# Gate and up weights of an FFN loaded in one piece into free residual buffers, last sums in place, two more places for weight forms

## The chip, the core and the metric

The kernel runs on one core of a Trainium2 chip: TensorE (PE) multiplies, VectorE (DVE), ScalarE (ACT) and GpSimd (POOL) do the rest, and SyncE (SP) issues the DMAs from one queue that is worked off in order. Each engine, too, works through its own list in order. The metric is the device time of one execution in microseconds: the median of three runs of the kernel before is 1670.28 (1666.36 to 1670.28).

## The reference

One decoder layer over 1024 tokens of width 1024, in float32: a mixer (eight retention heads beside four differential-attention heads), a memory cross-attention with four heads, and a SwiGLU feed-forward with 2816 hidden columns. All sub-layers are residual behind an RMS norm. The change touches the last of them:

```python
h = rms_norm(x, norm_ffn[l])
x = x + (jax.nn.silu(h @ w_gate[l]) * (h @ w_up[l])) @ w_down[l]
```

## The kernel before

Each float32 operand is split into a rounded high part and the rest as a low part, and a product is three matmuls (high by high, high by low, low by high) that add up in PSUM. The feed-forward saves one product in eight by a Strassen-Winograd scheme: operands are cut into quarters, sums of the quarters are formed, and seven products f1 to f7 take the place of eight.

The token side (`b_sums`, `b_part`) is prepared while the cross-attention ends. For each group p of 256 tokens the normed rows `xn_f` (L772) are summed (`bs`, L829), transposed by TensorE (`bt`) and split (`Bh`, `Bl`, `B4` to `B6`, L849 and L89).

The gate/up loop then runs over 22 hidden blocks j of 128 columns. `Forms(j)` (L1019) loads the raw gate and up block, 512 KB each, into two of the three buffers of the pool `st`; `sums` (L1033) builds sums of quarters in `sa` and `sb` on VectorE; `form` (L1028) turns each of the seven operands into a high part (a cast on ScalarE, L1030) and a low part (a subtraction, L89, on GpSimd or for f6 and f7 on VectorE). All seven go into the pool `w` with nine places. `GU.prod` issues the twelve matmuls of one product and `GU.after` (L1098) takes results out of PSUM: ScalarE copies one PSUM bank (`U` L1107, `G` L1112 and L1116), VectorE adds the other (`G`, `U`, L1013), ScalarE applies SiLU, GpSimd multiplies the second half of `G` (L1121) and VectorE the first (L1123). In one step TensorE's order is product 1 of block j+1, 7 of j, 2 of j+1, 4 of j, 5, 6 and 3 of j+1. Banks of one PSUM tile `xz` hold several products, so product 5 waits for the add that ends product 2, product 7 for the add that ends product 3, and product 6 for the copy `U` of product 5.

After every second block `g_forms` (L1068) forms the activations' sums `gSa` and `gSb` (tiles of the pool `xn`, two places) and stores them to `gF_d`. Also every second block `w_forms` (L1050) loads two raw blocks of the down weights into `st`, forms four sums in two tiles `wTa` and `wTb` of the pool `t4` (six places), and stores them to `wT_d`. The down projection behind the loop reads both back (`ds`), splits and multiplies them, and adds the residual, which was saved in `res_d` and is loaded into four 1 MB tiles `res` of the pool tag "B". Two of the four B places hold `B4` through the loop; the other two are free once the residual rows that were in them are normed.

TensorE's order is the order of the code. For the other engines and the DMA queue a scheduler chooses the order at build time: it takes whichever instruction it thinks ready first, with the earlier in the code preferred, and hands out pool places as they come free. A change of pools therefore moves instructions on every engine but TensorE.

Of the kernel before, what the change touches and what calls it, by code (L numbers as in the profile page):

```python
# [9 lines left out]
F32 = mybir.dt.float32  # L10
F32R = mybir.dt.float32r
# [5 lines left out]
P = 128  # L17
# [13 lines left out]
U_RET, U_DIF, U_OUT, U_KV, U_XQ, U_XO, U_GU, U_DN = 0, 16, 28, 36, 52, 60, 68, 112  # L31
# [6 lines left out]
def body(ctx, tc, a, out):  # L38
    nc = tc.nc
    ve, sc, gp, sp = nc.vector, nc.scalar, nc.gpsimd, nc.sync  # L40
# [15 lines left out]
    up = ctx.enter_context(tc.tile_pool(name="up", bufs=NW))  # L56
# [3 lines left out]
    drp = ctx.enter_context(tc.tile_pool(name="drp", bufs=1, space=bass.MemoryType.DRAM))  # L60
# [4 lines left out]
    def t4(name, dt=F32):  # L65
        return tp4.tile([P, 1024], dt, tag="t4", name=name)
# [20 lines left out]
    def low(eng, dst, src, hi):  # L87

        eng.tensor_tensor(out=dst, in0=src, in1=hi.bitcast(F32), op=ALU.subtract)  # L89

    def raw(name):
        return stp.tile([P, 1024], F32, tag="st", name=name)
# [173 lines left out]
    for i in range(2):  # L266
        r = c1.tile([P, P], F32, tag=f"R{i}", name=f"R{i}")
# [38 lines left out]
    class Ret:  # L306
        def __init__(self, g, w):
            self.g, self.w = g, w
            self.msk = c1.tile([P, 2, P], F32, tag="msk", bufs=2, name=f"msk{g}")
            sp.dma_start(self.msk, a["msk"][:, g])  # L310
            self.xi = c1.tile([P, P], F32, tag="xi", bufs=2, name=f"xi{g}")
            sp.dma_start(self.xi, a["xi"][:, g])
            self.o, self.rg = t4b(f"ro{g}"), t4b(f"rg{g}")
            self.st = {}
# [437 lines left out]
    bp = p2.enter_context(tc.tile_pool(name="bp", bufs=1))  # L752
    xr2 = [bp.tile([P, 2, D], F32, tag="B", bufs=4, name=f"xr{t}") for t in range(4)]
    xr = [xr2[t // 2][:, t % 2] for t in range(NT)]
    xnp = p2.enter_context(tc.tile_pool(name="xnp", bufs=2))
# [7 lines left out]
    def xnp_tile(name):  # L763
        return xnp.tile([P, 1024], F32, tag="xn", name=name)

    def normed(t, grow, name, pool=None):

        r = small(1, "rn", f"r_{name}")
        xn = (pool or xnp_tile)(f"xn_{name}")
        sc.activation(xn, xr[t], AF.Square, accum_out=r)  # L770
        rsqrt(r, 1, 1.0 / D, name)
        ve.scalar_tensor_tensor(out=xn, in0=xr[t], scalar=r, in1=grow, op0=ALU.mult, op1=ALU.mult)  # L772
        return xn
# [26 lines left out]
    for c in range(2):  # L800
        u = [unit(U_OUT + 4 * c + i, f"wo{c}_{i}", eng=ve if i % 2 else gp, pool=ntp if c and i < 2 else None)
             for i in range(4)]
        for t in range(NT):
# [8 lines left out]
            xn = normed(t, grow, f"x{t}", pool=t4 if t % 2 else None)  # L812
# [199 lines left out]
    def add(eng, dst, x, y):  # L1012
        eng.tensor_tensor(out=dst, in0=x, in1=y, op=ALU.add)  # L1013

    def sub(eng, dst, x, y):
        eng.tensor_tensor(out=dst, in0=x, in1=y, op=ALU.subtract)  # L1016


    class Forms:  # L1019
        def __init__(self, j):  # L1020
            self.j, self.fs = j, {}
            self.g, self.u = (raw(f"gu{j}_{i}") for i in range(2))
            sp.dma_start(self.g, a["w"][U_GU + 2 * j])
            sp.dma_start(self.u, a["w"][U_GU + 2 * j + 1])
            self.form(1, self.g[:, 0:512], gp)
            self.form(2, self.g[:, 512:1024], gp)

        def form(self, f, src, eng):  # L1028
            self.fs[f] = t = up.tile([P, 2, 512], F32R, tag="w", name=f"f{f}_{self.j}")
            sc.copy(t[:, 0], src)  # L1030
            low(eng, t[:, 1], src, t[:, 0])

# [15 lines left out]
    wT = {}  # L1048

    def w_forms(p):  # L1050

        r1, r2 = (raw(f"wd{p}_{i}") for i in range(2))
        for i, r in enumerate((r1, r2)):
            sp.dma_start(r, a["w"][U_DN + 2 * p + i])
        x, y = t4(f"wTa{p}"), t4(f"wTb{p}")
        B11, B12, B21, B22 = r1[:, 0:512], r1[:, 512:1024], r2[:, 0:512], r2[:, 512:1024]
        sub(ve, x[:, 0:512], B12, B11)
        sub(ve, x[:, 512:1024], B22, x[:, 0:512])
        sub(ve, y[:, 0:512], B22, B12)
        sub(ve, y[:, 512:1024], B21, x[:, 512:1024])  # L1060
        d = drp.tile([2, P, 1024], F32, tag=f"wT{p}", name=f"wT_d{p}")
        sp.dma_start(d[0], x)
        sp.dma_start(d[1], y)
        wT[p] = d

    gF, Gs = {}, {}

    def g_forms(p):  # L1068

        g1, g2 = Gs.pop(2 * p), Gs.pop(2 * p + 1)  # L1070
        A11, A21, A12, A22 = g1[:, 0:512], g1[:, 512:1024], g2[:, 0:512], g2[:, 512:1024]
        x, y = xnp_tile(f"gSa{p}"), xnp_tile(f"gSb{p}")
        d = drp.tile([4, P, 1024], F32, tag=f"gF{p}", name=f"gF_d{p}")
        sp.dma_start(d[0][:, 0:512], A11)
        sp.dma_start(d[1], g2)
        add(ve, x[:, 0:512], A21, A22)
        sub(ve, x[:, 512:1024], x[:, 0:512], A11)
        sub(ve, y[:, 0:512], A11, A21)
        sub(ve, y[:, 512:1024], A12, x[:, 512:1024])
        sp.dma_start(d[2], x)  # L1080
        sp.dma_start(d[3], y)
        gF[p] = d

    class GU:
# [13 lines left out]
        def after(self, f, c=slice(0, 512)):  # L1098
            X, Z = self.xz[:, c], self.xz[:, 512 + c.start:512 + c.stop]
            if self.G is None and f == 2:  # L1100
                self.G = t4(f"G{self.j}")
            if self.U is None and f == 5:
                self.U = hfp.tile([P, 512], F32, tag="xsq" if self.j % 2 else "xp", bufs=1, name=f"U{self.j}")
            if f == 1 or f in (6,) or (f != 5 and self.G is None):
                return
            if f == 5:
                sc.copy(self.U[:, c], Z)  # L1107
                return
            G1, G2 = self.G[:, c], self.G[:, 512 + c.start:512 + c.stop]
            U = self.U[:, c] if self.U is not None else None  # L1110
            if f == 2:
                sc.copy(G1, self.y[:, c])  # L1112
                add(ve, G1, X, G1)
                sc.activation(G1, G1, AF.Silu)
            if f == 3:
                sc.copy(G2, Z)  # L1116
                add(ve, G2, X, G2)
                sc.activation(G2, G2, AF.Silu)
            if f == 7:
                add(ve, U, X, U)  # L1120
                gp.tensor_tensor(out=G2, in0=G2, in1=U, op=ALU.mult)  # L1121
            if f == 4:
                ve.tensor_tensor(out=G1, in0=X, in1=G1, op=ALU.mult)  # L1123
                Gs[self.j] = self.G
                if self.j % 2 and c.stop == 512:
                    g_forms(self.j // 2)
# [31 lines left out]
    for j in range(NH):  # L1158
        n = GU(j + 1) if j + 1 < NH else None
        if n:  # L1160
            n.forms.sums()
            n.go(1)
        o.go(7, c1 if j == 0 else call_)
        if n:
            n.go(2)
        o.go(4, c1 if j == 0 else call_)
        if j % 2 == 0:
            w_forms(j // 2)
        if n:
            n.go(5)  # L1170
            n.prod(6)
            n.go(3)
        o = n
# [6 lines left out]
    X = [xs_[i // 2][:, 512 * (i % 2):512 * (i % 2) + 512] for i in range(4)]  # L1180
    Y = [(mm, ms)[i // 2](f"dy{i}") for i in range(4)]
    gsrc = {1: (0, 0), 2: (1, 0), 4: (1, 1), 5: (2, 0), 6: (2, 1), 7: (3, 0), 3: (3, 1)}
    wsrc = {5: (0, 0), 6: (0, 1), 7: (1, 0), 4: (1, 1)}

    outs = {1: [(X, 0, 0)], 2: [(Y, 0, 0, 1)], 6: [(X, 0, 1)], 5: [(Y, 1, 1)], 7: [(X, 1, 1, 1)],
            3: [(Y, 0, 1, 1)], 4: [(X, 1, 0, 1)]}
# [1 line left out]
    for f in (1, 2, 6, 5, 7, 3, 4):  # L1188
        bank = Y if f in (2, 5, 3) else X
        for p in range(NP):  # L1190
            s_ = raw(f"ds{f}_{p}")
            d, x = gsrc[f]
            sp.dma_start(s_[:, 0:512], gF[p][d][:, h5_(x)])
            if f in wsrc:
                d, x = wsrc[f]
# [10 lines left out]
        for b_, e, c, *last in outs[f]:  # L1206
            for i in range(4):
                t = 2 * i + e
# [74 lines left out]
def build(arrays):  # L1283
    nc = bacc.Bacc("TRN2", target_bir_lowering=False, num_devices=1, dynamic_dma_scratch_size=1024)
    aps = {k: nc.dram_tensor(f"in_{k}_dram", v.shape, mybir.dt.from_np(v.dtype), kind="ExternalInput").ap()
           for k, v in arrays.items()}
    out = nc.dram_tensor("out_0_dram", (NT, P, D), F32, kind="ExternalOutput").ap()
    with tile.TileContext(nc) as tc:
        with ExitStack() as ctx:
            body(ctx, tc, aps, out)  # L1290
    return nc
# [10 lines left out]
```

## Time and profile before

| | |
|---|---|
| median of three runs | 1670.28 us |
| the profiled execution | 1660.91 us, of it 1659.1 between first and last instruction |
| mean granted TensorE clock in it | 0.985 |
| busy: TensorE, VectorE, ScalarE, GpSimd | 93%, 60%, 37%, 25% |
| entry to the loop | about 941 to 1012 us |
| gate/up loop, steps 1 to 20 | 1012.49 to 1430.26 us |
| down projection | 1446.20 us to the end |

The page gives shares over the whole span, where stages have different limits. A change of one stage is read from the rows of that stage: what TensorE waited for there, and what chain of work ended that wait. The start of product 6 (the one behind the `U` copy) marks a step well, because TensorE always stops there for a moment. In the rows by stretch, what stands behind the length is the busy time of TensorE, of its weight loads (PEld), of VectorE, ScalarE and GpSimd, each with its count of instructions, and then the granted TensorE clock, the DMA engines' busy share and GB/s.

### The profile page before, as it was taken

The numbers are of one execution on the slowest core, as the hardware profiler recorded it, in microseconds if no ns is written. First come the engines' busy times: TensorE is split into PE (matmuls) and PEld (weight loads), VectorE is DVE, ScalarE is ACT, GpSimd is POOL, SyncE is SP. The second block draws the span as 40 slices with busy tenths as digits, with TensorE's granted clock in tenths as the row PEclk, the third lists the DMA queues.
The fourth block names the chain that finished last, engine by engine and source line by source line (L and its number), as shares of the span: only waits on it lengthen the run. The fifth ranks groups of instructions, "written<-read, shape, count | busy, mean of one in ns | idle before, by whom it ended". The sixth has DMA issues, their size and how long they took to land.

```text
span 1659.1 us, 23264 instructions
## 1 busy us (share of the span) xinstructions
PE 1549.4 (93%) x8712; PEld 1317.8 (79%) x8712; DVE 995.7 (60%) x2473; ACT 616.5 (37%) x1187; POOL 421.7 (25%) x343
## 2 busy tenths in 40 slices
PE   6899899899899999899999869999999999899998
PEld 5778878878888878798998767777777777788887
DVE  8955864864866724766676884444444444455554
ACT  5542442442445522332332443333333333333332
POOL 4323223223303411111121234433333333100000
PEclk8999999999999999999999989999999999999999
DMA  8201011111104552100011133444444444576664
GB/s 283 71 26 52 31 39 39 44 39 39 40 14 140 192 177 77 39 26 26 26 64 37 67 115 131 143 148 144 143 146 144 144 146 146 197 238 217 195 221 155
DMA packets 68417, 180.84 MB, mean 109 GB/s; under 512 B 7632, under 2 KB 13136, under 8 KB 68304
## 3 DMA queue, kind: packets, MB, share of 16 engines
q1 hardware_dynamic: 67296, 178.81, 31.6%
q8 instruction: 68, 1.11, 0.3%
q10 hardware_dynamic: 1008, 0.55, 0.1%
q14 instruction: 45, 0.37, 0.1%
HBM read 135.55 MB, written 43.78 MB: 108 GB/s over the span
## 4 chain that ended last, share of the span: by engine, by line
PE 63%; DVE 21%; DMA 6%; ACT 4%; issue 3%; POOL 3%; SPq 0%; POOLq 0%; ACTq 0%; DVEq 0%
PE xz L47 12%; PE g_r L47 8%; PE dx L47 7%; PE dy L47 5%; PE wo L47 5%; PE xo L47 5%; PE xq L47 4%; PE kv L47 3%; DMA gu<-in_w_dram 3%; PE q L47 2%; PE y L47 2%; PE av L47 2%; DVE sb L1016 1%; PE rsk L47 1%; DVE nmx L522 1%
## 5 line engine op out<-in xcount | busy, mean ns | idle before, releaser
L47 PE MATMUL xz<-Bh,f 128*128 128x512 f32 (+1 forms) x552 | 173.3, 386 | 7.5 <-DVE G L1013 7.4
L47 PE MATMUL g_r<-uh_r,xT 128*128 128x512 f32 x512 | 178.9, 407 | 0.0
L89 DVE TENSOR_TENSOR dl<-ds,dh 128x1024 fp32r<-128x1024 f32 x77 | 94.3, 1224 | 102.5 <-PE dy L47 36.7
L1200 ACT CAST dh<-ds 128x1024 fp32r<-128x1024 f32 x77 | 81.1, 1053 | 138.8 <-DMA ds<-wT_d 57.0
L47 PEld LDWEIGHTS xz<-Bh,f 128*128 128x128 f32 x552 | 103.0, 189 | 32.6 <-DVE G L1013 12.4
L47 PE MATMUL kv<-uh_d,xT 128*128 128x256 f32 x512 | 113.0, 303 | 5.4 <-DVE dql L445 5.4
L47 PEld LDWEIGHTS g_r<-uh_r,xT 128*128 128x128 f32 x512 | 97.0, 189 | 22.3 <-issue 2.5
L89 POOL TENSOR_TENSOR f<-gu,f 128x512 fp32r<-128x512 f32 x66 | 87.6, 1341 | 106.4 <-ACT f L1030 106.4
L47 PE MATMUL xz<-Bl,f 128*128 128x512 f32 (+1 forms) x276 | 105.3, 382 | 0.0
L47 PE MATMUL g_r<-ul_r,xT 128*128 128x512 f32 x256 | 101.0, 395 | 0.0
L47 PEld LDWEIGHTS kv<-uh_d,xT 128*128 128x128 f32 x512 | 88.8, 201 | 8.0 <-DVE dql L445 5.6
L47 PE MATMUL xq<-hT,uh_xq 128*128 128x256 f32 x512 | 94.4, 286 | 0.0
L47 PE MATMUL xo<-uh_xo,xoT 128*128 128x512 f32 x256 | 89.7, 409 | 2.1 <-DVE B6l L89 1.6
L525 ACT ACTIVATE p<-s,nmx,dsm 128x128 f32<-128x128 f32 (+7 forms) x64 | 53.2, 832 | 97.1 <-DVE nmx L523 96.4
L47 PEld LDWEIGHTS xq<-hT,uh_xq 128*128 128x128 f32 x512 | 81.1, 195 | 0.0
L47 PE MATMUL xz<-B6h,f 128*128 128x512 f32 (+1 forms) x184 | 61.4, 397 | 17.7 <-ACT U L1107 17.7
L47 PE MATMUL kv<-ul_d,xT 128*128 128x256 f32 x256 | 75.1, 293 | 2.4 <-DVE ul_d L89 2.4
L47 PE MATMUL xq<-hT,ul_xq 128*128 128x256 f32 x256 | 73.1, 285 | 0.0
L47 PE MATMUL dx<-dh 128*128 128x512 f32 x176 | 68.6, 390 | 0.4 <-DVE G L1123 0.4
L89 POOL TENSOR_TENSOR f<-sa,f 128x512 fp32r<-128x512 f32 x22 | 33.6, 1525 | 139.2 <-issue 77.4
L47 PE MATMUL dx<-dl,dh 128*128 128x512 f32 x176 | 68.5, 389 | 0.0
L47 PE MATMUL dx<-dh,dl 128*128 128x512 f32 x176 | 68.5, 389 | 0.0
(333 smaller groups left out, 4125.5 us busy)
## 6 DMA issues: line engine op xcount, KB each, us to landing
gu<-in_w_dram SPq DMA_DIRECT2D x44, 512.0 KB, 3.7
ds<-gF_d SPq DMA_DIRECT2D x77, 256.0 KB, 3.9
wd<-in_w_dram SPq DMA_DIRECT2D x22, 512.0 KB, 4.0
ds<-wT_d SPq DMA_DIRECT2D x44, 256.0 KB, 4.3
ds<-in_w_dram SPq DMA_DIRECT2D x33, 256.0 KB, 4.0
st_r<-in_w_dram SPq DMA_DIRECT2D x16, 512.0 KB, 3.3
st_kv<-in_w_dram SPq DMA_DIRECT2D x16, 512.0 KB, 3.4
st_d<-in_w_dram SPq DMA_DIRECT2D x12, 512.0 KB, 3.4
```

The costliest lines, as they stand in the source:

```text
L47: return tc.keep_in_program_order(nc.tensor.matmul(*args, **kw))
L89: eng.tensor_tensor(out=dst, in0=src, in1=hi.bitcast(F32), op=ALU.subtract)
L522: ve.tensor_reduce(out=nmx[:, m:m + 1], in_=s[:, :n], axis=AX.X, op=ALU.max, negate=True)
L525: sc.activation(pt[:, :n], s[:, :n], AF.Exp, bias=nmx[:, m:m + 1], scale=rq[:, m:m + 1], accum_out=Z[:, m:m + 1])
L1016: eng.tensor_tensor(out=dst, in0=x, in1=y, op=ALU.subtract)
L1200: sc.copy(hi, s_)
```

## The change

Three edits. The raw gate and up blocks of j >= 1 come as one load into one B place instead of two `st` buffers; block 0 stays as it was. The forms f3 and f7 of j >= 1 go into the two places of `xn`, whose former users `gSa` and `gSb` move to `t4`. `w_forms` makes its four sums in place, in the `st` buffers that were loaded, so `t4` loses `wTa` and `wTb`; the four sums land in another order, hence the new `wsrc`.

```diff
--- before.py
+++ after.py
@@ -1019,14 +1019,20 @@
     class Forms:
         def __init__(self, j):
             self.j, self.fs = j, {}
-            self.g, self.u = (raw(f"gu{j}_{i}") for i in range(2))
-            sp.dma_start(self.g, a["w"][U_GU + 2 * j])
-            sp.dma_start(self.u, a["w"][U_GU + 2 * j + 1])
+            if j:
+                gu = bp.tile([P, 2, 1024], F32, tag="B", bufs=4, name=f"gu{j}")
+                self.g, self.u = gu[:, 0], gu[:, 1]
+                sp.dma_start(gu, a["w"][U_GU + 2 * j:U_GU + 2 * j + 2].rearrange("i p c -> p i c"))
+            else:
+                self.g, self.u = (raw(f"gu{j}_{i}") for i in range(2))
+                for i, t in enumerate((self.g, self.u)):
+                    sp.dma_start(t, a["w"][U_GU + 2 * j + i])
             self.form(1, self.g[:, 0:512], gp)
             self.form(2, self.g[:, 512:1024], gp)
 
         def form(self, f, src, eng):
-            self.fs[f] = t = up.tile([P, 2, 512], F32R, tag="w", name=f"f{f}_{self.j}")
+            pool, tag = (xnp, "xn") if self.j and f in (3, 7) else (up, "w")
+            self.fs[f] = t = pool.tile([P, 2, 512], F32R, tag=tag, name=f"f{f}_{self.j}")
             sc.copy(t[:, 0], src)
             low(eng, t[:, 1], src, t[:, 0])
 
@@ -1049,19 +1055,17 @@
 
     def w_forms(p):
 
-        r1, r2 = (raw(f"wd{p}_{i}") for i in range(2))
-        for i, r in enumerate((r1, r2)):
-            sp.dma_start(r, a["w"][U_DN + 2 * p + i])
-        x, y = t4(f"wTa{p}"), t4(f"wTb{p}")
-        B11, B12, B21, B22 = r1[:, 0:512], r1[:, 512:1024], r2[:, 0:512], r2[:, 512:1024]
-        sub(ve, x[:, 0:512], B12, B11)
-        sub(ve, x[:, 512:1024], B22, x[:, 0:512])
-        sub(ve, y[:, 0:512], B22, B12)
-        sub(ve, y[:, 512:1024], B21, x[:, 512:1024])
-        d = drp.tile([2, P, 1024], F32, tag=f"wT{p}", name=f"wT_d{p}")
-        sp.dma_start(d[0], x)
-        sp.dma_start(d[1], y)
-        wT[p] = d
+        r = [raw(f"wd{p}_{i}") for i in range(2)]
+        for i in range(2):
+            sp.dma_start(r[i], a["w"][U_DN + 2 * p + i])
+        B11, B12, B21, B22 = r[0][:, 0:512], r[0][:, 512:1024], r[1][:, 0:512], r[1][:, 512:1024]
+        sub(ve, B11, B12, B11)
+        sub(ve, B12, B22, B12)
+        sub(ve, B22, B22, B11)
+        sub(ve, B21, B21, B22)
+        wT[p] = drp.tile([2, P, 1024], F32, tag=f"wT{p}", name=f"wT_d{p}")
+        for i in range(2):
+            sp.dma_start(wT[p][i], r[i])
 
     gF, Gs = {}, {}
 
@@ -1069,7 +1073,7 @@
 
         g1, g2 = Gs.pop(2 * p), Gs.pop(2 * p + 1)
         A11, A21, A12, A22 = g1[:, 0:512], g1[:, 512:1024], g2[:, 0:512], g2[:, 512:1024]
-        x, y = xnp_tile(f"gSa{p}"), xnp_tile(f"gSb{p}")
+        x, y = t4(f"gSa{p}"), t4(f"gSb{p}")
         d = drp.tile([4, P, 1024], F32, tag=f"gF{p}", name=f"gF_d{p}")
         sp.dma_start(d[0][:, 0:512], A11)
         sp.dma_start(d[1], g2)
@@ -1180,7 +1184,7 @@
     X = [xs_[i // 2][:, 512 * (i % 2):512 * (i % 2) + 512] for i in range(4)]
     Y = [(mm, ms)[i // 2](f"dy{i}") for i in range(4)]
     gsrc = {1: (0, 0), 2: (1, 0), 4: (1, 1), 5: (2, 0), 6: (2, 1), 7: (3, 0), 3: (3, 1)}
-    wsrc = {5: (0, 0), 6: (0, 1), 7: (1, 0), 4: (1, 1)}
+    wsrc = {5: (0, 0), 7: (0, 1), 4: (1, 0), 6: (1, 1)}
 
     outs = {1: [(X, 0, 0)], 2: [(Y, 0, 0, 1)], 6: [(X, 0, 1)], 5: [(Y, 1, 1)], 7: [(X, 1, 1, 1)],
             3: [(Y, 0, 1, 1)], 4: [(X, 1, 0, 1)]}
```

TensorE's order is unchanged. On the others the scheduler's order moves.

VectorE, in the step that ends a pair (names carry the block's number: `G12` is block 12's activation, `U11` block 11's, `gSa5` and `gSb5` pair 5's sums). Before:

```order
L1013 TENSOR_TENSOR G11_12355<-xz11_12294,G11_12355 128x512
L89 TENSOR_TENSOR f7_12_12453<-sb12_12439,f7_12_12453 128x512
L1013 TENSOR_TENSOR U11_12397<-xz11_12294,U11_12397 128x512
L1013 TENSOR_TENSOR gSa5_12514<-G10_12215,G11_12355 128x512
L1016 TENSOR_TENSOR gSb5_12515<-G10_12215 128x512
L1016 TENSOR_TENSOR gSa5_12514<-gSa5_12514,G10_12215 128x512
L1013 TENSOR_TENSOR G12_12497<-xz12_12436,G12_12497 128x512
L1013 TENSOR_TENSOR sa13_12578<-gu13_1_12567 128x512
```

And now:

```order
L1013 TENSOR_TENSOR G11_12323<-xz11_12262,G11_12323 128x512
L1013 TENSOR_TENSOR U11_12363<-xz11_12262,U11_12363 128x512
L89 TENSOR_TENSOR f7_12_12417<-sb12_12403,f7_12_12417 128x512
L1013 TENSOR_TENSOR gSa5_12478<-G10_12185,G11_12323 128x512
L1013 TENSOR_TENSOR G12_12461<-xz12_12400,G12_12461 128x512
L1016 TENSOR_TENSOR gSa5_12478<-gSa5_12478,G10_12185 128x512
L1016 TENSOR_TENSOR gSb5_12479<-G10_12185 128x512
L1013 TENSOR_TENSOR sa13_12540<-gu13_12530 128x512
L1127 TENSOR_TENSOR G11_12323<-xz11_12262,G11_12323 128x512
```

The add `G12<-xz12,G12`, which product 5 of block 12 waits for, stood behind three gS sums and stands behind one.

GpSimd, in the same step (`f2_13` is the low part of block 13's form 2). Before:

```order
L89 TENSOR_TENSOR f3_12_12449<-sb12_12439,f3_12_12449 128x512
L89 TENSOR_TENSOR f4_12_12456<-gu12_1_12427,f4_12_12456 128x512
L89 TENSOR_TENSOR f1_13_12570<-gu13_0_12566,f1_13_12570 128x512
L89 TENSOR_TENSOR f2_13_12573<-gu13_0_12566,f2_13_12573 128x512
L1121 TENSOR_TENSOR G11_12355<-G11_12355,U11_12397 128x512
```

And now:

```order
L89 TENSOR_TENSOR f5_12_12405<-sa12_12402,f5_12_12405 128x512
L89 TENSOR_TENSOR f4_12_12420<-gu12_12392,f4_12_12420 128x512
L89 TENSOR_TENSOR f1_13_12532<-gu13_12530,f1_13_12532 128x512
L89 TENSOR_TENSOR f2_13_12535<-gu13_12530,f2_13_12535 128x512
L89 TENSOR_TENSOR f3_12_12413<-sb12_12403,f3_12_12413 128x512
L1125 TENSOR_TENSOR G11_12323<-G11_12323,U11_12363 128x512
```

The product `G11` stood behind block 13's f1 and f2; they are now ahead of f3.

VectorE, at the entry to the loop (`xn_f6` and `xn_f7` are the last two normed rows, `rw`, `ry`, `rx` and `r` small steps of their scale, `wd` the raw down weights). Before:

```order
L145 SCALAR_TENSOR_TENSOR ry_f7_10649<-rw_f7_10650,ry_f7_10649 128x1
L140 SCALAR_TENSOR_TENSOR rw_f7_10650<-ry_f7_10649,rx_f7_10648 128x1
L145 SCALAR_TENSOR_TENSOR ry_f7_10649<-rw_f7_10650,ry_f7_10649 128x1
L140 SCALAR_TENSOR_TENSOR rw_f7_10650<-ry_f7_10649,rx_f7_10648 128x1
L145 SCALAR_TENSOR_TENSOR r_f7_10645<-rw_f7_10650,ry_f7_10649 128x1
L772 SCALAR_TENSOR_TENSOR xn_f7_10646<-xr3_6924,r_f7_10645,g_ffn_9641 128x1024
L1013 TENSOR_TENSOR G0_10541<-xz0_10499,G0_10541 128x256
L829 TENSOR_TENSOR bs3_1_10662<-xn_f7_10646,xn_f6_10591 128x512
L89 TENSOR_TENSOR Bl_10179<-bt3_1_10731,Bh_10180 128x4x128
```

And now:

```order
L1016 TENSOR_TENSOR wd0_1_10961<-wd0_1_10961,wd0_0_10960 128x512
L140 SCALAR_TENSOR_TENSOR rw_f6_10595<-ry_f6_10594,rx_f6_10593 128x1
L132 TENSOR_SCALAR rx_f7_10648<-r_f7_10645 128x1
L1016 TENSOR_TENSOR wd0_1_10961<-wd0_1_10961 128x512
L145 SCALAR_TENSOR_TENSOR r_f6_10590<-rw_f6_10595,ry_f6_10594 128x1
L133 TENSOR_SCALAR r_f7_10645<-r_f7_10645 128x1
L772 SCALAR_TENSOR_TENSOR xn_f6_10591<-xr3_6924,r_f6_10590,g_ffn_9641 128x1024
L134 TENSOR_SCALAR ry_f7_10649<-r_f7_10645 128x1
L1016 TENSOR_TENSOR wd1_0_11236<-wd1_0_11236 128x512
L136 TENSOR_SCALAR ry_f7_10649<-ry_f7_10649 128x1
L140 SCALAR_TENSOR_TENSOR rw_f7_10650<-ry_f7_10649,rx_f7_10648 128x1
L1013 TENSOR_TENSOR G0_10541<-xz0_10499,G0_10541 128x256
```

Sums of `wd0` and `wd1` stand among the steps of `xn_f6` and `xn_f7`, and the add `G0` has moved ahead of `xn_f7`; the `U0` add and two `Bl` follow it there, not shown. Further on all eleven pairs of `wd` sums stand before the eighth step (before: one pair every second step up to the last). In SyncE's queue each `wd` load now stands behind the store of the tile whose buffer it takes, each gate/up load (`gu11` and `gu12` behind the stores of pair 3) a step or two ahead of its use, and the loads of `res0` and `res1` have moved from the entry to behind `gu21`.

## Rows read from the trace of the kernel before

**Rows 1.** TensorE's line of the page's part 1, and the traffic of part 2's 40 slices.
```profile
PE 1549.4 (93%) x8712; PEld 1317.8 (79%) x8712; DVE 995.7 (60%) x2473; ACT 616.5 (37%) x1187; POOL 421.7 (25%) x343
...
GB/s 283 71 26 52 31 39 39 44 39 39 40 14 140 192 177 77 39 26 26 26 64 37 67 115 131 143 148 144 143 146 144 144 146 146 197 238 217 195 221 155
```

**Rows 2.** What TensorE waited for from 1020 to 1400: us in total, times, longest.
```profile
PE xz L47 <- ACT U L1107: 13.1, 18, 0.7
PE xz L47 <- DVE G L1013: 6.8, 17, 1.1
```

**Rows 3.** Busy time of each engine by stretch; start:end, length, then engine by engine.
```profile
941.00:1012.49 71.49, 53.67 (x334) 46.98 (x334) 50.28 (x105) 31.35 (x59) 26.01 (x20) 0.93 0.25 90
1012.49:1138.05 125.56, 118.57 (x505) 93.69 (x505) 61.27 (x84) 41.96 (x72) 49.65 (x36) 1.00 0.42 148
1138.05:1430.26 292.21, 276.69 (x1176) 218.56 (x1176) 141.82 (x198) 98.40 (x168) 111.75 (x82) 1.00 0.43 148
1076.45:1096.67 20.22, 19.49 (x84) 15.69 (x84) 7.60 (x11) 5.78 (x10) 6.75 (x5) 1.00 0.42 145
1096.67:1117.83 21.16, 20.05 (x85) 15.54 (x85) 12.57 (x18) 8.17 (x15) 9.64 (x7) 1.00 0.44 150
...
1446.20:1659.10 212.90, 208.37 (x918) 172.28 (x918) 106.86 (x102) 75.81 (x72) 0.00 (x0) 1.00 0.63 209
```

**Rows 4.** Timeline of TensorE, 1050 to 1100: start, length, operation, idle time before and releaser.
```profile
1063.85 0.50 PE L47 MATMUL xz<-Bh,f 128*128 128x512 f32 x1 [0.45 <-DVE G L1013]
...
1072.73 0.50 PE L47 MATMUL xz<-B5h,f 128*128 128x512 f32 x1 [0.37 <-DVE G L1013]
```

**Rows 5.** Chain of waits, 1180 to 1224: start us, us, what.
```profile
1178.01 5.03 DMA gu<-in_w_dram
...
1187.29 0.59 ACT G L1116
...
1187.90 0.70 DVE G L1013
...
1192.39 1.28 POOL f L89
1193.68 1.26 POOL G L1121
...
1196.86 0.61 DVE G L1013
```

**Rows 6.** What SyncE's DMA queue waited for, 1000 to 1440.
```profile
SPq L1024 <- DVE sb L1016: 65.3, 10, 6.8
```

**Rows 7.** VectorE's groups by form, 1020 to 1400: busy us, mean ns, idle time before, releaser.
```profile
L1016 DVE TENSOR_TENSOR sb<-gu,sa 128x512 f32<-128x512 f32 x18 | 25.7, 1429 | 0.3
...
L1016 DVE TENSOR_TENSOR wTa<-wd,wTa 128x512 f32<-128x512 f32 x9 | 13.5, 1505 | 0.0
...
L1013 DVE TENSOR_TENSOR sa<-gu 128x512 f32<-128x512 f32 x18 | 12.4, 687 | 43.0 <-DMA gu<-in_w_dram 43.0
...
L1016 DVE TENSOR_TENSOR sb<-gu,gu 128x512 f32<-128x512 f32 x18 | 12.3, 684 | 0.0
```

**Rows 8.** DMA issues, 1020 to 1400: count, size of each, median us to landing.
```profile
gu<-in_w_dram SPq DMA_DIRECT2D x36, 512.0 KB, 4.3
wd<-in_w_dram SPq DMA_DIRECT2D x19, 512.0 KB, 3.4
...
wT_d<-wTa SPq DMA_DIRECT2D x9, 512.0 KB, 2.6
```

**Rows 9.** Timeline of TensorE at the entry to the loop.
```profile
984.46 0.39 PE L47 MATMUL xz<-Bh,f 128*128 128x256 f32 x1 [2.47 <-DVE G L1013]
...
995.18 0.39 PE L47 MATMUL xz<-B5h,f 128*128 128x256 f32 x1 [0.92 <-DVE G L1013]
```

**Rows 10.** Timeline of VectorE at the entry to the loop.
```profile
979.50 1.29 DVE L772 SCALAR_TENSOR_TENSOR xn_f<-xr,r_f,g_ffn 128x1024 f32<-128x1024 f32 x1
...
982.79 1.28 DVE L772 SCALAR_TENSOR_TENSOR xn_f<-xr,r_f,g_ffn 128x1024 f32<-128x1024 f32 x1
```

## The prediction

> **What bounds the kernel now.** I read the page first [rows 1]: TensorE is busy 93% of the span, so only its idle stretches can be won. The waits of TensorE inside the gate/up loop [rows 2] leave two releasers, ScalarE's copy `U` (L1107) and VectorE's add `G` (L1013). The table by stretch [rows 3] gives the sizes. One step j of the loop (84 matmuls, seven products of 12, some 2.78 us each: 19.49 busy over seven) takes 20.22 us where only the `U` copy is waited for, and 21.16 where the add is too. The 20 steps from 1012.49 to 1430.26 are two rows there: the first six took 125.56 us, the other fourteen 292.21. Against 20.22 a step (121.32 and 283.08) that is 4.24 and 9.13 us over. The down projection behind 1446 has TensorE at 208.4 of 212.9 us and touches none of the changed orders: I count it as fixed.
>
> The timeline of TensorE [rows 4] shows the two add waits of a pair of steps: 0.45 us ahead of product 7 and 0.37 ahead of product 5 (a refilled pipe costs a little more). The chain [rows 5] says where they come from. Ahead of product 7: a `gu` half that lands 5.03 us after its issue, the sums made from it, ScalarE's copy (0.59), then the add at 1187.90. Ahead of product 5: the low part of the following step's f2 on GpSimd (1.28 us), then the product `G` (1.26), then three gS sums, then the add at 1196.86. Both chains start in the three `st` buffers and nine `w` places. The queue of SyncE [rows 6] agrees: the second `gu` half (L1024) waits 65.3 us for VectorE's sums to give a buffer back.
>
> **The change part by part.** *Gate and up as one load into the residual buffers.* Two B places are free from about 984 on, so load j+2 waits only for the forms and sums of load j, not for `wd` sums. SyncE's order after shows `gu11` and `gu12` a step or two ahead of use, so VectorE's 43.0 us of waiting ahead of `sa` [rows 7] goes. What was late because of it is the `G` add behind the sums (product 7). The next thing late is the add's own input, ScalarE's copy: it follows the end of product 3 and is 2.78 us early, the length of the product between. A 1 MB load isn't in the trace: from below it costs what a half costs (4.3 us median [rows 8]), from above two halves (8.6). I take 5.5, nearest to one half, since two halves issued together share the queue. With a step of 20.22 us ahead both ends cost nothing.
>
> *f3 and f7 in `xn`.* Five forms instead of seven share the nine `w` places, so the following step's f1 and f2 find a place around product 5, not behind product 1 of that step. GpSimd's order has f2 ahead of f3 now, and f3, whose input is ready when product 3 ends, right ahead of the product `G`; it is done before product 7 is. Counted from the end of product 7: `U` add 0.7, `G` product 1.3, `gSa` 0.7, so `gSa` ends at about 2.8 us; ScalarE's copy of `y` ends at 3.4 (a product and 0.59); the add at 4.1. Product 5 is due at 5.6 (two products). The order on VectorE also moves the add from behind three gS sums to behind one. So the wait ahead of product 5 goes, with 1.5 us to spare.
>
> *What the later fourteen steps give.* All of it is 9.13 us. In one of two steps ScalarE now casts f6 and f4 between VectorE's second sum and the `U` copy, and both come just in time: the copy may start a tenth or two late (0.14 in seven steps is 1.0). I leave 1.0 of the gain behind: minus 8.1 (ends: minus 9.1, and 0 if the waits stay).
>
> *`wd` sums in place.* The number of sums stays at four a pair. But they are no longer tied to free `t4` places, and the scheduler draws all eleven pairs forward: wd0 to wd2 stand ahead of or inside the entry to the loop, wd3 to wd9 in steps 1 to 6. There VectorE has them at 0.68 us each (0.60 from start to start), or 1.5 where GpSimd reads beside it [rows 7]. A `wd` tile now holds its `st` buffer until its store has landed: sum, store 2.6, next load 3.4 [rows 8], some 7 us a round for three buffers, or a pair in 5 us where a step takes 20. In bytes: 1.05 MB of gate/up, 0.92 of `gF`, and 7 pairs over 5.5 steps times 2.1 MB, 2.67: 4.64 MB in 20.22 us, 230 GB/s, where the loop moved 148 [rows 3] and the first slice of the page 283 [rows 1]. It fits, but a sum that waits for its load holds the `G` add behind it. So of the first six steps' 4.24 us I take half: minus 2.1 (ends: minus 4.2, and plus 18, the second rival).
>
> The row shows more on collisions: `sb<-gu,sa` takes 1429 ns and its twin `sb<-gu,gu` 684 [rows 7]. [...] VectorE is busy 7.6 to 12.6 of a step [rows 3], so the sum stays and only the second rival's chance grows.
>
> *The entry to the loop.* Before it VectorE is the slow engine: 50.3 of 71.5 us from 941 to 1012, TensorE 53.7 with a granted clock of 0.93 [rows 3]. The order puts three wd0 sums ahead of `xn_f6`, and one wd1 sum, the `G` add, two `Bl` and the `U` add ahead of `xn_f7`. `xn_f6` moves from 979.50 [rows 10] to about 981.3 (3 x 0.60). Product 7 waited until 984.46 for an add that stood behind `xn_f7` [rows 9]; the add is now ahead of it and product 7 starts at about 984.1, a little earlier. But `xn_f7` slides from 982.79 [rows 10] to about 987 (the `U` add ahead of it needs product 7's end), and its transposes, which stood behind product 7 anyway, by some 1.6. Product 5 of the next quarter, at 995.18 [rows 9], waits for an add behind two or three more sums. I count plus 1.5 (ends: minus 0.5, if the earlier product 7 keeps TensorE ahead; plus 4.8, seven sums at 0.68, all on the path).
>
> *Nothing:* the first wd0 sum falls where VectorE waits for an exponential; `res0` and `res1`, now loaded at step 20, are first read 30 us into the down projection; the `ds` casts at the end stand earlier, while the waits behind 1430.26 come from products that follow each other directly: that stretch stays.
>
> The sum on the profiled execution, 1660.91 us (span 1659.1 plus 1.8): -8.1 - 2.1 + 1.5 = -8.7, that is 1652.2. The shown runs lie 9.4 us higher (median 1670.28), and the change should come on top of that: 1661.6 us.
>
> **The rivals.** *The add stays late.* One gS sum still stands ahead of it, and it is released by GpSimd. For this: that pair of products was the chain before too [rows 5]. Against: f2 no longer stands ahead. If GpSimd ends 1.4 us later than I count, the 0.94 us (21.16 less 20.22) of seven steps come back, 6.6, the early steps give nothing, and the entry costs 1.5: 1670.28 - 9.1 + 1.0 + 6.6 + 1.5 = about 1670.
>
> *VectorE waits for `wd` loads, slower than before.* Place: steps 1 to 6 and the entry. Price: a wait like those ahead of `sa`: 43.0 us over 18 [rows 7], in every second step, 4.8 each, less a product of 2.78 that covers it, 2.0 us; once a pair for wd2 to wd10, 18 us: 1670.28 - 8.1 + 1.5 + 18 = 1682. It decides once a `wd` load lands more than 2.8 us after VectorE reaches its sum. For it: the trace has just such waits for loads issued behind stores. Against: 230 of 283 GB/s, and 5 us for a pair in a step of 20.
>
> *All of it goes:* 13.4 us less and an entry at no cost, 1657; it lies in the forecast's own range.
>
> **How the numbers follow.** Forecast 0.62 (own range 1656 to 1667), the add stays late 0.23, VectorE waits for `wd` 0.15. A measurement of this kernel tells a change from none at about 0.3%, 5.0 us: faster is below 1665.3, slower above 1675.3. Faster: 0.58 of the first and 0.02 of the second, 0.60; the rest of the first, 0.21 of the second and 0.02 of the third, 0.27 the same; the rest of the third, 0.13, slower. The range 1655 to 1674 leaves out most of the `wd` case and a sliver of the first.
>
> **What would show it.** In the profile after: a step near 20.2 to 20.4 us from the eighth on, TensorE's waits for `G` L1013 in the loop near nothing, those for `U` still 0.73 each; VectorE idle ahead of `wd` sums in steps 1 to 6 at under 2.8 us each; the loop's first f6 at 1013 to 1015. The forecast is wrong if steps 1 to 6 take over 21.5 us, if GpSimd's `G` still stands late ahead of `gSa`, or if the entry slides by more than 5 us.

## The result: 0.5% slower, lost at the entry and in the first four steps

The changed kernel takes 1676.80 us (median of 6 runs, 1674.92 to 1681.66) against 1669.46 (6 runs) before: ratio 1.0054, 95% interval 1.0035 to 1.0072, some 9 us by the ratio and 7.3 by the medians. Forecast was 1661.6. The profiled execution took 1680.02 us, of it 1678.0 between first and last instruction.

The page of the changed kernel, the lines that answer to [rows 1]:

```profile
PE 1563.5 (93%) x8712; PEld 1331.5 (79%) x8712; DVE 1048.5 (62%) x2473; ACT 615.5 (37%) x1187; POOL 444.1 (26%) x343
...
GB/s 279 70 26 51 31 38 43 39 38 39 39 13 157 202 143 87 28 26 26 26 64 51 51 188 234 225 236 108 94 95 95 94 95 98 147 247 221 191 220 156
```

TensorE does the same 8712 matmuls and is busy 14.1 us longer: part of the loss is matmuls at a lower granted clock (0.974 in the mean of this execution), not only idle time. The traffic has a hump of 225 to 236 GB/s around the first steps, and less than before behind it.

The table by stretch of the changed kernel; a step is again counted from one product 6 behind a `U` copy to the next, and the columns are those of [rows 3] (the first row is the last part of the entry, from the product 6 at 982.54 to the one at 1025.34; then steps 1 to 6, steps 7 to 20, one step of these, and the rest):

```profile
982.54:1025.34 42.80, 33.98 (x196) 30.94 (x197) 30.96 (x54) 14.35 (x29) 13.55 (x11) 0.84 0.62 227
...
1025.34:1164.33 138.99, 124.40 (x504) 97.69 (x504) 93.26 (x104) 41.37 (x73) 59.58 (x38) 0.95 0.59 204
1164.33:1449.83 285.50, 275.27 (x1176) 219.62 (x1176) 153.59 (x166) 96.49 (x166) 121.17 (x80) 1.00 0.29 102
1205.12:1225.51 20.39, 19.66 (x84) 15.69 (x84) 8.36 (x12) 6.44 (x12) 7.61 (x6) 1.00 0.32 116
1449.83:1678.00 228.17, 221.38 (x972) 182.26 (x972) 112.11 (x109) 79.10 (x76) 1.29 (x1) 1.00 0.60 200
```

Steps 1 to 6 take 138.99 us where [rows 3] have 125.56: 13.4 lost. Steps 7 to 20 take 285.50 for 292.21: 6.7 won, all fourteen alike at 20.39. The entry part took 35.5 before: 7.3 lost. Here 196 matmuls keep TensorE busy 33.98 us at a granted clock of 0.84. The row of before for it:

```profile
976.95:1012.49 35.54, 30.14 (x196) 27.25 (x196) 21.23 (x41) 12.24 (x24) 10.16 (x9) 0.95 0.30 105
```

What TensorE waited for in the loop (1026 to 1410), which answers to [rows 2]:

```profile
PE xz L47 <- ACT U L1111: 13.3, 18, 0.8
PE xz L47 <- DVE G L1013: 8.0, 3, 4.7
PE xz L47 <- DVE U L1013: 2.1, 1, 2.1
```

The small add waits of every second step are gone; four long ones have come, all in the first four steps. The timeline of TensorE at the four (answering to [rows 4]), with matmuls behind the first and the second, and the same kind of matmul 6 us later:

```profile
1041.56 0.51 PE L47 MATMUL xz<-B4h,f 128*128 128x512 f32 x1 [2.09 <-DVE U L1013]
...
1043.29 1.05 PE L47 MATMUL xz<-B4h,f 128*128 128x512 f32 x2
...
1071.35 0.80 PE L47 MATMUL xz<-B5h,f 128*128 128x512 f32 x1 [4.69 <-DVE G L1013]
1071.94 0.63 PE L47 MATMUL xz<-B5l,f 128*128 128x512 f32 x1
1072.37 1.05 PE L47 MATMUL xz<-B5h,f 128*128 128x512 f32 x2
...
1078.01 0.63 PE L47 MATMUL xz<-B6h,f 128*128 128x512 f32 x2
...
1095.75 0.50 PE L47 MATMUL xz<-B5h,f 128*128 128x512 f32 x1 [1.42 <-DVE G L1013]
...
1109.96 0.50 PE L47 MATMUL xz<-Bh,f 128*128 128x512 f32 x1 [1.91 <-DVE G L1013]
```

Behind 4.69 us of idling two matmuls take 1.05 us instead of 0.63: the granted clock is 0.50 until about 1076. The same follows the waits of 2.09 and 1.91 us, for some 3 to 4 us each (0.50 from 1042.5 to 1045.5 and from 1111 to 1113), and not the one of 1.42 (1.00 from 1095.7 to 1101): steps 1, 2 and 4 have TensorE busy for 21.51, 22.24 and 21.44 us, where an undisturbed step has 19.66. The chain of waits ahead of the longest (answering to [rows 5]) says what the add stood behind:

```profile
1054.84 0.61 DVE wd L1016
...
1055.47 7.05 DMA wT_d<-wd
...
1062.54 3.60 DMA wd<-in_w_dram
...
1066.16 0.70 DVE wd L1016
...
1066.88 2.52 DMA wT_d<-wd
...
1069.40 0.69 DVE wd L1016
1070.09 0.60 DVE sa L1013
1070.69 0.60 DVE G L1013
```

A sum in place, its store (7.05 us), the next load into the same buffer (3.60), the next sum: VectorE stands still in front of that sum, with the `G` add behind it in its list. The waits of 2.09 and 1.91 us end the same way, behind an add that stands directly behind late `wd` sums; ahead of the one of 1.42 other sums stand between. VectorE's waits, the longest of them, then SyncE's (1026 to 1140; [rows 6] for SyncE), and the DMA landings of 1026 to 1150 ([rows 8]):

```profile
DVE wd L1016 <- DMA wd<-in_w_dram: 19.7, 5, 6.2
```

```profile
1038.76 1.42 DVE L1016 TENSOR_TENSOR wd<-wd,wd 128x512 f32<-128x512 f32 x2 [6.24 <-DMA wd<-in_w_dram]
```

```profile
SPq L1068 <- DVE wd L1016: 24.8, 14, 3.7
SPq L1060 <- DMA wT_d<-wd: 24.7, 12, 4.8
```

```profile
wT_d<-wd SPq DMA_DIRECT2D x16, 512.0 KB, 5.9
wd<-in_w_dram SPq DMA_DIRECT2D x13, 512.0 KB, 4.9
gu<-in_w_dram SPq DMA_DIRECT2D x6, 1024.0 KB, 6.3
```

Loads wait for stores (L1060), stores for sums (L1068), and a round that the prediction put at 7 us takes 0.7 + 5.9 + 4.9, over 11.

The entry, by VectorE's timeline (answering to [rows 10]), then by TensorE's (answering to [rows 9]):

```profile
983.21 0.68 DVE L1016 TENSOR_TENSOR wd<-wd,wd 128x512 f32<-128x512 f32 x1
...
986.64 1.28 DVE L772 SCALAR_TENSOR_TENSOR xn_f<-xr,r_f,g_ffn 128x1024 f32<-128x1024 f32 x1
...
992.52 1.85 DVE L772 SCALAR_TENSOR_TENSOR xn_f<-xr,r_f,g_ffn 128x1024 f32<-128x1024 f32 x1
```

```profile
988.07 1.94 PE L51 MATMUL bt<-ident,xn_f 128*128 128x128 f32 x8 [2.41 <-DVE ry_f L134]
...
994.42 1.10 PE L51 MATMUL bt<-ident,xn_f 128*128 128x128 f32 x4 [2.47 <-DVE xn_f L772]
...
1005.38 0.58 PE L47 MATMUL xz<-B5h,f 128*128 128x256 f32 x1 [2.65 <-DVE G L1013]
```

This execution is 5.59 us behind the one of before at the first product 6 shown (982.54 for 976.95). Against that, `xn_f6` comes 1.6 us later than in [rows 10] and `xn_f7` 4.1. TensorE waits for the transposes' rows twice, 2.41 us until `xn_f6` is done (the small step `ry_f` named there stands right behind it) and 2.47 for `xn_f7`, and 2.65 ahead of product 5. Behind each of the three a part of its matmuls runs at a lower clock: granted were 0.50 from 988 to 990, 0.53 from 996 to 998 and 0.50 from 1006 to 1010. The wait of 2.47 us that product 7 had in [rows 9] is gone.

### The profile page after: what moved, and what is told of

Its sections match the earlier page's. It is cut to its first block, busy times and chain, and to the rows that moved or that the text cites. A ratio compares the mean times of both kernels' runs of the same rounds, so it can differ in the third digit from the quotient of the medians.

```text
span 1678.0 us, 23222 instructions
## 1 busy us (share of the span) xinstructions
PE 1563.5 (93%) x8712; PEld 1331.5 (79%) x8712; DVE 1048.5 (62%) x2473; ACT 615.5 (37%) x1187; POOL 444.1 (26%) x343
## 4 chain that ended last, share of the span: by engine, by line
PE 67%; DVE 18%; DMA 5%; ACT 4%; issue 3%; POOL 3%; ACTq 0%; SPq 0%; DVEq 0%; POOLq 0%
PE xz L47 16%; PE g_r L47 8%; PE dx L47 7%; PE dy L47 5%; PE wo L47 5%; PE xo L47 5%; PE xq L47 4%; PE kv L47 3%; PE q L47 2%; PE y L47 2%; PE av L47 2%; DMA wT_d<-wd 1%; PE rsk L47 1%; POOL f L89 1%; PE s L47 1%
## 5 line engine op out<-in xcount | busy, mean ns | idle before, releaser
L89 DVE TENSOR_TENSOR dl<-ds,dh 128x1024 fp32r<-128x1024 f32 x77 | 94.3, 1224 | 100.4 <-PE dy L47 38.6
L47 PEld LDWEIGHTS g_r<-uh_r,xT 128*128 128x128 f32 x512 | 96.4, 188 | 22.3 <-issue 2.5
L89 POOL TENSOR_TENSOR f<-gu,f 128x512 fp32r<-128x512 f32 x66 | 102.0, 1568 | 33.3 <-ACT f L1036 32.4
L1013 DVE TENSOR_TENSOR G<-xz,G 128x512 f32<-128x512 f32 (+1 forms) x46 | 30.7, 667 | 79.1 <-ACT G L1120 73.1
L47 PE MATMUL xz<-B5h,f 128*128 128x512 f32 (+1 forms) x184 | 62.4, 403 | 8.8 <-DVE G L1013 8.8
```

The source lines that it names most:

```text
L47: return tc.keep_in_program_order(nc.tensor.matmul(*args, **kw))
```

## The experiments

The theory (A): in place, a `wd` sum needs no `t4` place any more, and with gate/up out of the `st` buffers nothing else holds the pairs back; drawn forward, they put VectorE, which works in order, behind loads that wait for stores. Rivals: gate/up load or `xn` forms cost it (B), traffic or the mere number of sums (G), or the clock of the entry alone (E). C, D and F belong to single runs and stand in their expectations.

**A second profile of before.** The unchanged kernel. 

> The kernel before once more, for a second profile of it. If the 9 us between the first profile (1660.91) and the median (1669.5) lie in the granted clock of stretches ahead of the loop, this profile has the same steps (20.22 and 21.2 to 21.6) and another start of step 1 than 1012.49, by up to 9 us. If they lie in the loop, the steps differ.

1666.41 us, ratio 0.9995 (0.9983 to 1.0006).

```profile
984.89:1020.60 35.71, 30.16 (x197) 26.93 (x197) 21.03 (x41) 12.25 (x24) 10.19 (x9) 0.95 0.32 105
```

The loop repeats (step 1 to 6 took 125.65 us, 7 to 20 took 290.65), the entry too, and its first product 6 stands 7.9 us later than in the first profile. So the low 1660.91 was won ahead of the rows compared here. Beside this row the changed kernel's entry has 3.8 us more of busy TensorE for the same matmuls (clock 0.84 for 0.95) and 3.3 more of idling.

**Sums out of place again.** The changed kernel with

```diff
-        sub(ve, B11, B12, B11)
...
+        x, y = t4(f"wTa{p}"), t4(f"wTb{p}")
+        sub(ve, x[:, 0:512], B12, B11)
...
```

> The changed kernel with the wd sums in two tiles of t4 again, as before the change (gate/up load in one piece and f3, f7 in xn kept). Theory A: the pairs stand in every second step again, because t4 places pace them; entry as before, steps about 20.4 us, about 1660. Rival B (gate/up load or xn forms cost the entry): about 1676. Rival D (t4, which now holds gSa and gSb beside wTa and wTb, runs short): steps of 21 us and over, 1667 or more.

1657.12 us, ratio 0.9940 (0.9928 to 0.9953).

```profile
1019.97:1142.33 122.36, 117.98 (x505) 94.11 (x505) 74.46 (x86) 41.64 (x73) 56.47 (x37) 1.00 0.42 151
1142.33:1427.84 285.51, 275.28 (x1177) 219.64 (x1177) 168.25 (x196) 98.03 (x168) 124.54 (x82) 1.00 0.42 152
```

All twenty steps at 20.39, and an entry of 36.58 us (983.39 to 1019.97). One edit undone turns plus 0.5% into minus 0.6%; B falls, since neither of its parts costs this by itself, and so does D, since `t4` doesn't run short. Against these 117.98 us the changed kernel's steps 1 to 6 were 6.4 busier (clock 0.95) and idled 10.2 more, which are the four waits of 10.1: all of its 16.6.

**All pairs held until the loop.**

```diff
+        if p == 0:
+            gate.append(cp.tile([P, 1], F32, name="gate"))
+            sc.copy(gate[0], o.G[:, 0:1])
         for i in range(2):
+            sc.copy(r[i][:, 0:1], gate[0])
             sp.dma_start(r[i], a["w"][U_DN + 2 * p + i])
```

> The changed kernel with all wd loads held until block 0's G is copied, so that none stands in the entry; from there on they come as fast as the three buffers allow. Theory A: the entry is as before (minus 9 us of the profile), VectorE still waits some 15 to 20 us for wd loads in steps 1 to 7 and those steps take 2 to 3 us each too much: about 1668 to 1671. Rival E (the steps were slow because the entry had lowered TensorE's clock): clock 1.00 behind 1012, steps 20.4 to 21, about 1660.

1670.05 us, 1.0021 (1.0004 to 1.0037).

```profile
983.11:1020.07 36.96, 30.47 (x197) 26.97 (x197) 28.65 (x47) 14.95 (x35) 12.96 (x11) 0.95 0.47 166
1020.07:1153.29 133.22, 119.67 (x505) 93.59 (x505) 90.91 (x112) 43.55 (x90) 64.71 (x38) 1.00 0.69 245
```

The entry is back to 37 us, the first six steps still lose 10.9 against out_of_place, at a granted clock of 1.00: two separate losses, and E falls.

**Each pair held until its own step.** Here the gate is the block's own G, `sc.copy(r[i][:, 0:1], o.G[:, 0:1])` ahead of each load. 

> The changed kernel, with one tiny ScalarE copy of a column of the block's own G into each raw wd tile ahead of its load, so that no wd load or sum can be drawn ahead of its own pair of steps. Theory A (the in-place sums drawn forward, each holding its buffer through its store, cost the entry and steps 1 to 6, about 26 us of the profile; the rest of the change gives 0.5 us a step): entry as before (product 6 of step 1 at 1012 to 1016), all twenty steps at 20.4 us, VectorE's wait for wd loads in the loop under 3 us in all, 1669.5 - 10 = about 1660 (1656 to 1664). Rival B (the 1 MB gate/up load or the forms in xn cost at the entry): entry and first steps stay slow, about 1676. Rival C (sums back in every second step bring the G add waits back): entry as before, steps alternate 20.4 and 21.2, about 1667.

1674.57 us, 1.0049 (1.0035 to 1.0062): theory A was wrong about this cure. VectorE's waits in the loop:

```profile
DVE wd L1016 <- DMA wd<-in_w_dram: 65.5, 18, 7.4
```

Steps 1 to 6 were fine (123.60), but later the gated load starts too late for the place that its sum has in VectorE's list, and TensorE waits up to 1.7 us for the add behind that sum in six of the later steps (295.04 for steps 7 to 20):

```profile
1145.98 1.57 DVE L1016 TENSOR_TENSOR wd<-wd 128x512 f32<-128x512 f32 x1 [7.41 <-DMA wd<-in_w_dram]
```

```profile
1148.94 0.50 PE L47 MATMUL xz<-Bh,f 128*128 128x512 f32 x1 [1.69 <-DVE G L1013]
```

It is the same mechanism with another cause of the late load. The pattern is rival C's, undisturbed steps beside steps of 21.6 to 22.3. The rest behind the steps takes 233.69 us for 228.2; why wasn't followed up.

**The stores left out.** The changed kernel, with only pair 0's sums stored and read.

```diff
+        if p:
+            wT[p] = wT[0]
+            return
         wT[p] = drp.tile([2, P, 1024], F32, tag=f"wT{p}", name=f"wT_d{p}")
```

> The changed kernel, but only pair 0's wd sums are stored, and the down projection reads pair 0's for all pairs (20 stores of 512 KB, 10.5 MB, are left out; the sums are still made). The sums stand even closer together, in the entry and steps 1 to 4. Theory A (the round sum, store, next load makes VectorE wait): VectorE's waits for wd loads of 12 to 20 us fall below 5, steps 1 to 6 below 21.3 us on average; the entry stays as late as with the change: about 1666 (1662 to 1670). Rival G (the burden of so many sums beside GpSimd, or the traffic of the loads): steps 1 to 6 stay at 22 to 27 us, about 1674 or more.

1672.24 us, 1.0027 (1.0014 to 1.0040); entry 42.04. Steps 1 to 6, then VectorE's waits (1010 to 1440):

```profile
1023.22:1154.39 131.17, 120.51 (x505) 94.95 (x505) 88.28 (x98) 41.45 (x73) 60.08 (x38) 0.99 0.41 145
```

```profile
DVE wd L1016 <- DMA wd<-in_w_dram: 14.4, 6, 3.7
```

Between the theories: 7.8 of the 16.6 us lost in steps 1 to 6 go with the stores; waits for the loads remain, shorter ones. At 145 GB/s, no more than the loop moved before (148 [rows 3]), the total traffic can't be what is left; how much of the rest is waits and how much mere sums stays open.

**The parts one by one.** Each is the kernel before with that part of the diff alone. In place: 

> The kernel before with one edit: the wd sums in place. Gate/up still load into the same three buffers, so wd pairs can't be drawn forward. Theory A (an in-place sum holds its buffer through its store, and whoever needs the buffer next is late): gate/up loads now wait for wd stores too, VectorE waits longer for them than before (43 us over 18), steps of a pair at 20.2 and 22 or more, about 1675 (1670 to 1690). Rival F (in place costs nothing by itself, only the drawing forward does): the steps stay 20.2 and 21.2 to 21.6, about 1667.

1667.35 us, 0.9993 (0.9980 to 1.0006). A's forecast failed, F's held: VectorE waits 53.5 us for `wd` loads over 20 times here, and the steps hardly change (291.04 for 7 to 20), with the pairs spread over the whole loop: TensorE waits at most 1.0 us for an add.

One load of gate and up: 

> The kernel before with one edit: gate and up of block 1 on as one load into the residual buffers. The prediction's step: TensorE's add wait ahead of product 7 (0.2 to 0.6, 10 pairs) goes, that ahead of product 5 stays; steps 20.22 and 21.16, about 1666.6 - 4 = 1663. If the part gives nothing (the add is late by something else): 1666. If the 0.17 us by which every undisturbed step got longer (20.22 to 20.39) comes with the 1 MB load or its place: steps 20.39 and 21.3 here.

1657.70 us, 0.9942 (0.9920 to 0.9965): steps of 20.22 and 20.86; the add wait ahead of product 7 is gone, 0.39 us ahead of product 5 stays.

f3 and f7 in `xn`: 

> The kernel before with one edit: f3 and f7 of block 1 on in xn, gSa and gSb in t4. The prediction's step: TensorE's add wait ahead of product 5 (0.37 and a pipe to fill, 10 pairs) goes, that ahead of product 7 stays where it was; steps 20.22 and 20.5 to 20.8, about 1666.6 - 6 = 1661. If the 0.17 us of every undisturbed step comes with the places of f3 and f7: 20.39 here.

1661.00 us, 0.9952 (0.9935 to 0.9969).

```profile
1015.79:1138.13 122.34, 117.95 (x505) 94.14 (x505) 69.14 (x84) 41.79 (x72) 53.13 (x36) 1.00 0.43 152
```

Steps of 20.39 with no add wait at all, though VectorE still waits 42.4 us for gate/up loads (1020 to 1400). So either edit removes product 7's wait, and the 0.17 us a step comes with this one.

One load and in place: 

> The kernel before with two edits of the three: gate/up as one load into the residual buffers, and the wd sums in place; forms and gS sums as before. Theory A (the loss needs both: in place no longer asks for a t4 place, and the gate/up load no longer asks for an st buffer, so nothing paces the wd pairs): entry late by some 7 us, VectorE waits 15 us or more for wd loads, steps 1 to 6 at 130 us and over in sum, later ones 20.2 and 20.9: about 1673 to 1677. Rival B (the forms in xn are part of the loss): 1665 or less.

1668.44 us, 1.0014 (1.0000 to 1.0028).

```profile
980.45:1021.26 40.81, 32.74 (x196) 29.70 (x196) 30.46 (x54) 13.51 (x27) 13.01 (x10) 0.87 0.68 238
1021.26:1147.85 126.59, 118.23 (x505) 93.77 (x505) 79.87 (x104) 42.66 (x73) 51.37 (x36) 1.00 0.65 226
```

The entry is 4.0 us longer than gu_only's 36.79 and steps 1 to 6 are 3.5 longer than its 123.14; in place eats some 11 us of what the one load wins. Both theories missed on size: without the `xn` forms the waits are shorter (longest 3.7 us) and the clock of these steps stays at 1.00. So the size of the loss depends on all three edits. Why the waits are longer with these forms in `xn` isn't settled.

**Better versions.** The one load, with GpSimd's `G` product on VectorE: 

> The kernel before with gate and up of block 1 on as one load into the residual buffers, and the product of G's second half with U (block 1 on) on VectorE instead of GpSimd; nothing else of the change. If the remaining add wait ahead of product 5 (0.40 us in gu_only, step 20.86 against 20.22) hangs on GpSimd doing f1, f2 and then that product ahead of the gS sums, it goes: every step 20.22, 10 x 0.64 = 6.4 us below gu_only: about 1651. If VectorE's own extra 0.6 us a step delays the add as much: as gu_only, about 1657.5.

1659.97 us, 0.9958 (0.9941 to 0.9975); and with f2's low part there: 

> As gu_only, with the low part of f2 (block 1 on) on VectorE instead of GpSimd. GpSimd's product of G comes 1.3 us earlier, but in VectorE's order f2 stands right behind the U add, ahead of the gS sums. If the wait ahead of product 5 hangs on GpSimd's list it goes: steps 20.22, about 1651. If f2, whose place among the nine comes free late, holds VectorE up: steps over 20.9, 1658 or more.

1658.82 us, 0.9954 (0.9936 to 0.9971). Both keep a wait ahead of product 5 (0.29 and 0.23 us). Their twenty steps are a little shorter than gu_only's (408.3 and 409.2 us for 410.8), but the medians aren't lower: neither is shown to be better. Then out_of_place with one form in `xn` (`f == 3` or `f == 7` in place of `f in (3, 7)`): 

> As out_of_place, but of the forms only f3 goes to xn, f7 stays among the nine places. Every undisturbed step was 20.22 us with all forms in one pool and 20.39 with f3 and f7 in xn. If the longer step hangs on f7's place (product 7 rose most, 2.72 to 2.79): 20.22 to 20.27 here, and if eight places less one form still bring f2 in time, no add wait: about 1654. If it hangs on f3 (2.77 to 2.80) or on the shorter rotation of the nine places: 20.3 to 20.39, 1657. If one form less is not enough for f2: the 0.4 us wait ahead of product 5 is back in every second step, 20.8, as gu_only.

> As out_of_place, but of the forms only f7 goes to xn, f3 stays among the nine places. If the longer step hangs on f7's place: 20.3 to 20.39; if on f3's: 20.22 to 20.27. Add waits as in the twin: none (1654 to 1657) if one form less is enough, 0.4 us in every second step if not.

f3 alone: 1654.82 us, 0.9923 (0.9902 to 0.9944), the lowest median of all, though the interval overlaps those of out_of_place and gu_only; f7 alone: 1658.35, 0.9949 (0.9930 to 0.9968). Two starts of product 6 in the f3 kernel:

```profile
1183.12 0.50 PE L47 MATMUL xz<-B6h,f 128*128 128x512 f32 x1 [0.73 <-ACT U L1113]
1203.40 0.51 PE L47 MATMUL xz<-B6h,f 128*128 128x512 f32 x1 [0.73 <-ACT U L1113]
```

20.28 us, and 20.33 in the twin, with no add wait in either: f3's place costs 0.06 a step, f7's 0.11, together the 0.17. One form out of the nine places is enough.

## Why the prediction was wrong, step by step

- **Later fourteen steps, minus 8.1:** measured minus 6.7. No add wait is left, as said; the 1.0 us left behind for a late copy didn't come, but 0.17 x 14 = 2.4 us did, in the matmuls. The division was half right: gate/up and product 7, `xn` and product 5, but `xn` alone does both.
- **First six steps, minus 2.1:** measured plus 13.4. This is the step that failed: "sum, store 2.6, next load 3.4, some 7 us a round for three buffers, or a pair in 5 us where a step takes 20". Landing times were taken from a loop that moved 148 GB/s, with one pair in every second step; among the drawn-forward traffic they were 5.9 and 4.9, a round of over 11 us. And what a step has to spare on average doesn't help an add that stands behind a late load: VectorE waited 6.24 us for one, and TensorE 2.09 for the add behind it; two late loads (3.6 and 1.95) made the wait of 4.69. Of the 16.6 us lost against out_of_place, 10.2 are such idling and 6.4 the lower clock behind it, which stood in no term. The total traffic came out as estimated (204 GB/s in these steps for 230).
- **The entry, plus 1.5:** measured plus 7.3. The moved rows came out as counted (`xn_f6` 1.6 late for 1.8, `xn_f7` 4.1 for 4.2); what failed was the price. Product 7 stopped waiting, as forecast, but the transposes ahead of it and behind it waited 2.41 and 2.47 us (0.9 and nothing before), and the wait ahead of product 5 grew from 0.92 [rows 9] to 2.65: 3.4 us more of idling in all. The matmuls of the stretch ran at a clock of 0.84, which costs 3.8 us and stood in no term. That VectorE was the slow engine there doesn't follow from the row used for it, in which TensorE is busy longer (53.7 us for 50.3).
- **The rest, nothing:** 228.2 us behind the loop for 228.8.
- **The rivals.** "VectorE waits for `wd` loads", given 0.15, is what happened, in place and mechanism: VectorE waited 19.7 us, in five pieces up to 6.2, where the rival had nine of 4.8. Its price for TensorE, 18 us in nine pieces of 2.0, came as 13.4: four waits, 10.1 in sum, and the lower clock behind three of them, less the small waits that went. Its 1682 lies near the measured time partly by luck, since this price was too high and the entry's too low. "The add stays late" fell. The `wd` sums from 1026 to 1140 took 971 and 1043 ns in the mean where an undisturbed twin takes 684 [rows 7], some 10 us over 31 sums. The ten that took 1.2 to 1.8 us all started while a GpSimd instruction was running; of the other 21, at 0.68 to 0.69 us, one did. How much of the 10 us reached TensorE isn't shown.
- **The base.** The sum against the profiled execution was sound, since control shows that its 8 us of lead lie ahead of the rows compared. The sizes come from single profiles, though: the parts add up to some 13 us lost, the medians differ by 7.3.

## What to carry to other kernels

A pool that runs short can be what keeps optional work in its place; before freeing it, look at what the scheduler draws forward, and onto which in-order engine. In place saves a buffer only if the result is read on the spot: behind a store, the input buffer is held for sum, store and next load, over 11 us here. Cost a wait of an in-order engine by the latest single transfer and by what stands right behind it in the list, not by the mean: VectorE waited up to 7.4 us in paced and up to 5.5 in inplace_only, but TensorE at most 1.7 and 1.0 for an add in the loop. Then add what a lower granted clock behind TensorE's own wait costs, 6.4 us in the changed kernel's steps 1 to 6.

## What the runs showed of the hardware

In the changed kernel a wait of TensorE of 4.69 us was followed by about 5 us at a granted clock of 0.50, and waits of 2.09 and 1.91 us by some 3 to 4; the granted clock of steps 1 to 6 was 0.95 for 1.00, 6.4 us more of busy time for the same matmuls. A wait of 1.42 us there, and waits of up to 2.67 us in gate_first's first six steps, left it at 1.00. So the length of one wait alone doesn't tell whether the clock falls.

Weights in another pool made matmuls slower: with f3 and f7 in `xn`, in the changed kernel's steps 7 to 20, product 3 took 2.79 us instead of the 2.77 of before's undisturbed steps, 7 took 2.80 for 2.72, and the products behind them, 1 and 2, 2.75 for 2.72, with no wait shown. Whether it is the address or the neighbours' traffic wasn't settled.
